# Two more retention heads as seven-product pairs, with their norm in the output product and all head norms' sums on ScalarE

## The chip, the cores and the metric

One core of one Trainium2 chip runs the whole program in one launch. The metric is the device time of that core in microseconds (us), median of the runs shown; lower is better.

## The reference, cut to what matters

```python
# x is (1, 256, 2048) f32; layer 0 is GLA (4 heads), layer 1 retention (8 heads of 512 value columns)
def retention_mixer(h, positions, w_in, gn_g, gn_b, w_out):
    proj = h @ w_in                                   # 2048 -> 2048 q, 2048 k, 4096 v, 4096 gate
    q, k, v, gate = jnp.split(proj, [...], axis=-1)
    ...                                               # rotary, decayed causal scores
    o = ...                                           # scores @ v, per head (256, 512)
    mu = jnp.mean(o, axis=-1, keepdims=True)
    var = jnp.mean(jnp.square(o - mu), axis=-1, keepdims=True)
    o = ((o - mu) * lax.rsqrt(var + EPS)).reshape(B, S, D_INNER)
    o = o * gn_g + gn_b
    return (o * jax.nn.silu(gate)) @ w_out
# h = h + gla_mixer(rms_norm(h, g)); h = h + retention_mixer(rms_norm(h, g)); return rms_norm(h, g)
```

## The kernel before, in words

The 256 tokens stay on the chip and the f32 weights stream past them. A 1 MB "raw" chunk (four buffers, loaded by the SP queue, L192) is cut into two "units". ScalarE rounds a unit to fp32r (`hi`, L218) and VectorE takes the remainder (`lo`, L219), three buffers of each; they are numbered through the program, and the numbering is the order of the weights. A product of TensorE is three matmuls: x-high by hi, x-high by lo, x-low by hi (L358 to L360 in a pair, L267 to L269 in a group).

A plain group (`group_x`, L271) multiplies all 16 k-tiles by both token tiles for one 512-column block: 8 units and 96 matmuls of 512 columns. A seven-product pair (`pair_x`, L340) makes two such blocks together, in Strassen's manner: seven products S1 to S7, each over 4 k-tiles for both column blocks (2 units, 12 matmuls), and the other 8 k-tiles plainly as V0 to V3 and G0 to G3 (1 unit, 12 matmuls each). That is 180 matmuls and 22 units in place of 192 and 16. The sums of weight blocks are made by loads: seven 1 MB loads by SP, and eight 512 KB loads on POOL's queue that accumulate onto a chunk already split (L228, with `then`). A pair needs sums of the tokens as left operand: `token_sums` (L284, VectorE, `*_f` and `*_c`) and `token_parts` (L309, hi by ScalarE and lo by VectorE, `c*_d`).

The order of the blocks is written out by hand in the tables OUT, RET and END (L122 to L126). `plan_all` (L149) lays the units in that order before anything is emitted; `emit_split` (L198) issues splits two units ahead and loads two chunks ahead. Work of a head that is not its weight product waits as generators in the queue `side`; `advance` takes one step of it after each unit or block, and `drain_side` (called in an output pair before V2, as `late`) empties it. A scheduler then fixes each engine's order at build time. PSUM pools: `acc` 4 banks, `lev` 2, `mis` 2.

Retention heads come in two halves: heads 0 to 3 and the output pairs ra0 and ra1, heads 4 to 7 and rb0 and rb1. Each head (`ret_head`, L1242) first makes q and k (`rqk`, a group). Heads 0, 1, 2 and 4, 5, 6 then make value and gate as a pair (`rp0_` ... `rp6_`) in the order RET, and their attention output, norm and gate (`o_part`, `norm_part` L1279, `og_part` L1303) run during the next head's rqk, through `waiting`. Heads 3 and 7 make value and gate as two plain groups (`rv`, `rg`). Their norm runs during rg, from its third unit (`classic`, L1316), which also queues the token sums and splits for the output pairs (`ra_f`, `ra_c`, `c3_d`); their gate multiply and four transposes (`rot`, L692), with the two copies into the output operand `ogt` (L697 hi by ScalarE, L698 lo by VectorE), run at the start of ra0 and rb0, which follow the order OUT. The norm takes mean and variance by VectorE's batch-norm instructions (L1283, L1284) straight from PSUM, and then a scaled subtract (L1285), a Newton reciprocal root of nine tiny steps (`rsqrt`, L482), and a multiply and add.

## Time and profile before

| what | value |
|---|---|
| median of the three runs | 1378.68 us (1377.20 to 1379.46) |
| the profiled execution: its own time | 1378.59 us |
| the span that its trace covers | 1376.8 us |
| mean granted TensorE clock | 0.998 of full speed |
| busy share of the span: TensorE, its weight loads | 99%, 82% |
| busy share: VectorE, ScalarE, POOL | 80%, 60%, 12% |
| loaded and stored | 331.76 MB, mean 241 GB/s |

Busy shares are averages over the whole span. The time lies in the profiled execution 1.8 us outside the span, and 0.09 us below the median. "PE" in rows is TensorE, "PEld" its weight loads, DVE VectorE, ACT ScalarE. An idle time is shown in brackets with what ended it. Successive matmuls overlap, so the distance between the starts of two is their cost, and so it is for VectorE.

### The profile page before, as it was taken

Reading aid. Unit: us, or ns where it says so; the run is one execution under the profiler, and the core shown is the slowest. Engines: PE = TensorE matmul, PEld = TensorE weight load, DVE = VectorE, ACT = ScalarE, POOL = GpSimd, SP = SyncE. Lnnn points to the kernel's source line nnn. Section 1 sums busy time; section 2 is a strip of 40 time slices with the busy share of each in tenths; the row PEclk is TensorE's granted clock in tenths of the full one; section 3 lists DMA queues with packets and bytes.
Section 4 is the critical chain, followed back from the end, with each engine's and each line's share of the span. In section 5 each row is a group of like instructions: output and inputs, shape, how many; then the busy total and the mean of one; then the engine's idle time right before and its main releaser. Section 6 shows DMA issues by size and latency. Waiting matters only on the chain.

```text
span 1376.8 us, 17653 instructions
## 1 busy us (share of the span) xinstructions
PE 1360.3 (99%) x6500; PEld 1132.5 (82%) x6500; DVE 1104.7 (80%) x1517; ACT 831.9 (60%) x1060; POOL 171.9 (12%) x218
## 2 busy tenths in 40 slices
PE   8999999999999999999999999999999999999997
PEld 7888888788878888788888888888888888888876
DVE  6695896888797798887988888878758888887887
ACT  6676666655666766665665656455546465654665
POOL 1011110110122020111011111001201010100210
PEclk9999999999999999999999999999999999999999
DMA  9564785899899695699698969559989797964996
GB/s 366 204 245 163 208 250 186 191 290 321 231 266 277 183 268 195 178 263 278 192 293 265 293 201 286 188 186 262 255 336 226 260 236 251 244 245 163 225 300 168
DMA packets 58871, 331.76 MB, mean 241 GB/s; under 512 B 6928, under 2 KB 7440, under 8 KB 29856
## 3 DMA queue, kind: packets, MB, share of 16 engines
q1 hardware_dynamic: 34656, 238.96, 47.1%
q0 software_dynamic: 23408, 89.01, 33.1%
q10 hardware_dynamic: 720, 2.66, 0.5%
q8 instruction: 51, 0.84, 0.2%
q14 instruction: 36, 0.29, 0.1%
HBM read 324.31 MB, written 6.29 MB: 240 GB/s over the span
## 4 chain that ended last, share of the span: by engine, by line
PE 88%; DVE 5%; DMA 4%; issue 2%; ACT 1%; POOL 0%; ACTq 0%; POOLq 0%; DVEq 0%
PE rqk_ps L464 8%; PE rqk_ps L465 4%; DMA raw<-in_w_all 4%; PE rp__ps L359 4%; PE rp__ps L358 4%; PE rp__ps L360 4%; PE gqk_ps L464 2%; DVE lo L219 2%; PE gp__ps L359 2%; PE gp__ps L360 2%; PE gp__ps L358 2%; PE gv_ps L267 2%; PE gv_ps L268 2%; PE gv_ps L269 2%; PE gg_ps L268 2%; PE gg_ps L267 2%
## 5 line engine op out<-in xcount | busy, mean ns | idle before, releaser
L218 ACT ACTIVATE hi<-raw 128x1024 fp32r<-128x1024 f32 (+1 forms) x585 | 616.9, 1058 | 475.0 <-PE rqk_ps L464 69.0
L219 DVE TENSOR_TENSOR lo<-raw,hi 128x1024 fp32r<-128x1024 f32 (+1 forms) x585 | 709.8, 1223 | 231.3 <-ACT hi L218 222.7
L228 POOL DMA_DIRECT2D raw<-in_w_all x144 | 124.0, 861 | 645.4 <-DVE lo L219 442.5
L464 PE MATMUL rqk_ps<-xhl,hi 128*128 128x512 f32 x480 | 162.6, 397 | 0.0
L465 PE MATMUL rqk_ps<-xhl,lo 128*128 128x256 f32 x480 | 123.3, 281 | 0.0
L464 PEld LDWEIGHTS rqk_ps<-xhl,hi 128*128 128x128 f32 x480 | 88.2, 188 | 17.9
L465 PEld LDWEIGHTS rqk_ps<-xhl,lo 128*128 128x128 f32 x480 | 88.2, 189 | 3.6
L359 PE MATMUL rp__ps<-lo,xhl 128*128 128x512 f32 x192 | 74.9, 390 | 0.0
L360 PE MATMUL rp__ps<-hi,xhl 128*128 128x512 f32 x192 | 74.7, 389 | 0.0
L358 PE MATMUL rp__ps<-hi,xhl 128*128 128x512 f32 x192 | 69.8, 389 | 0.0
L359 PE MATMUL gp__ps<-lo,xhl 128*128 128x512 f32 x128 | 51.0, 399 | 1.5 <-DVE lo L219 1.5
L268 PE MATMUL gv_ps<-lo,xhl 128*128 128x512 f32 x128 | 50.9, 398 | 0.0
L268 PE MATMUL gg_ps<-lo,xhl 128*128 128x512 f32 x128 | 50.1, 392 | 0.0
L269 PE MATMUL gv_ps<-hi,xhl 128*128 128x512 f32 x128 | 50.0, 391 | 0.0
L360 PE MATMUL gp__ps<-hi,xhl 128*128 128x512 f32 x128 | 50.0, 390 | 0.0
L269 PE MATMUL gg_ps<-hi,xhl 128*128 128x512 f32 x128 | 49.8, 389 | 0.0
L464 PE MATMUL gqk_ps<-xhl,hi 128*128 128x512 f32 x144 | 49.6, 398 | 0.0
L358 PE MATMUL gp__ps<-hi,xhl 128*128 128x512 f32 x128 | 47.6, 393 | 0.0
L267 PE MATMUL gg_ps<-hi,xhl 128*128 128x512 f32 x128 | 46.7, 390 | 0.0
L267 PE MATMUL gv_ps<-hi,xhl 128*128 128x512 f32 x128 | 46.2, 393 | 0.0
L359 PEld LDWEIGHTS rp__ps<-lo,xhl 128*128 128x128 f32 x192 | 36.1, 188 | 7.5 <-DVE lo L219 0.3
L358 PEld LDWEIGHTS rp__ps<-hi,xhl 128*128 128x128 f32 x192 | 36.0, 188 | 7.5
(554 smaller groups left out, 2984.4 us busy)
## 6 DMA issues: line engine op xcount, KB each, us to landing
raw<-in_w_all SPq DMA_DIRECT2D x220, 1024.0 KB, 5.9
raw<-in_w_all POOLq DMA_DIRECT2D x144, 512.0 KB, 7.9
ogt<-xc POOLq DMA_DIRECT2D x2, 2048.0 KB, 10.8
resid<-in_x_n SPq DMA_DIRECT2D x2, 1024.0 KB, 10.9
xc<-ogt POOLq DMA_DIRECT2D x1, 2048.0 KB, 9.1
gg<-in_gn_g POOLq DMA_DIRECT2D x8, 256.0 KB, 4.0
gb<-in_gn_b POOLq DMA_DIRECT2D x8, 256.0 KB, 3.9
xc<-ogt ACTq DMA_DIRECT2D x1, 2048.0 KB, 7.3
```

Source lines behind the costliest of these rows:

```text
L218: a = nc.scalar.activation(hi[:, sl], src[:, sl], AF.Copy)
L219: b = nc.vector.tensor_tensor(lo[:, sl], src[:, sl], hi[:, sl].bitcast(F32), ALU.subtract)
L228: nc.gpsimd.dma_start(src, chunk_src(*then)[:, rows], accum_op=ALU.add)
L267: mm(ps, xh, hi[:, q, :], start=kt == 0, stop=False)
L268: mm(ps, xh, lo[:, q, :], start=False, stop=False)
L269: mm(ps, xl, hi[:, q, :], start=False, stop=kt == NKT - 1)
L358: mm(ps, xh, hi[:, q, :], start=start, stop=False, skip_group_check=True)
L359: mm(ps, xh, lo[:, q, :], start=False, stop=False, skip_group_check=True)
L360: mm(ps, xl, hi[:, q, :], start=False, stop=stop, skip_group_check=True)
L464: mm(ps[c], wh, rhs[:, kt, :, :], start=kt == 0, stop=False)
L465: mm(ps[c][:, 0, :], wl, rhs[:, kt, 0, :], start=False, stop=False)
```

## The change

Heads 3 and 7 become pairs too, in the order RET (`rp3_`, `rp7_`). The held gate multiply and transposes of heads 2 and 6 (`held`), the token sums and the first half of the token splits for the output run during that pair; its own norm, gate multiply and transposes run in ra0 and rb0, in the `mis` banks. These two output pairs follow a new order, LATE, which has V2 after S6, and G0 and G1 ahead of it; V2 is the first block that reads the transposed output of head 3 or 7. `load_fn` for columns 0 and 1 moves behind the drained side work. In all eight heads the mean is a ScalarE copy with an accumulated sum (into `o` in SBUF), and the variance a ScalarE square with the mean as bias, written over PSUM with an accumulated sum.

```diff
--- before.py
+++ after.py
@@ -122,6 +122,8 @@
     OUT = ("S1", "S2", "V0", "V1", "S5", "S3", "V2", "G0", "S6", "G1", "S7", "V3", "S4", "G2", "G3")
     RET = ("S1", "V0", "S2", "V1", "S5", "S3", "V2", "G0", "S6", "G1", "S7", "V3", "S4", "G2", "G3")
 
+    LATE = ("S1", "S2", "V0", "V1", "S5", "S3", "G0", "G1", "S6", "V2", "S7", "V3", "S4", "G2", "G3")
+
     END = ("S1", "S2", "V0", "V1", "S5", "S3", "V2", "V3", "G0", "S6", "G1", "G2", "G3", "S7", "S4")
 
     def plan_pair(gp, gq, order):
@@ -151,7 +153,7 @@
         for part, (stage, heads) in enumerate((("gla", 2), ("gla", 2), ("ret", 4), ("ret", 4))):
             for h in range(heads * part, heads * part + heads):
                 plan_group(g)
-                if stage == "ret" and h % heads < heads - 1:
+                if stage == "ret":
                     plan_pair(g + 1, g + 2, RET)
                     g += 3
                     continue
@@ -164,11 +166,10 @@
                         plan_group(g + 4)
                     g += 5
                     continue
-                rest = 4 if stage == "gla" else 2
-                for k in range(1, rest + 1):
+                for k in range(1, 5):
                     plan_group(g + k)
-                g += rest + 1
-            plan_pair(g, g + 1, OUT)
+                g += 5
+            plan_pair(g, g + 1, LATE if stage == "ret" else OUT)
             plan_pair(g + 2, g + 3, END if g + 4 == n_groups else OUT)
             g += 4
 
@@ -306,15 +307,17 @@
                 nc.vector.tensor_tensor(c[:, 1], a11, a21, ALU.add)
             yield
 
-    def token_parts(name, room, keep_in=None):
-        got = []
-        for half in range(2):
+    def token_parts(name, room, keep_in=None, halves=(0, 1)):
+        got = parts.setdefault(name, [])
+        for half in halves:
             c = sums[name][half]
             d = room(half)
             nc.scalar.activation(d[:, 0], c, AF.Copy)
             nc.vector.tensor_tensor(d[:, 1], c, d[:, 0].bitcast(F32), ALU.subtract)
             got.append(d)
             yield
+        if len(got) < 2:
+            return
         combos[name] = tuple((got[i][:, 0, k], got[i][:, 1, k]) for i, k in ((0, 0), (0, 1), (1, 0), (1, 1)))
         if keep_in is not None:
             nc.gpsimd.dma_start(keep_in, ogt[:, 2 * CHUNK :])
@@ -334,8 +337,7 @@
     def temps_t4(name):
         return t4_p.tile([P, CHUNK, SEQ], F32, tag="t4", name=name)
 
-    sums = {}
-    combos = {}
+    sums, parts, combos = {}, {}, {}
 
     def pair_x(lhs, name, cname, on, order, late=None, sparse=False, halves=False):
 
@@ -1001,6 +1003,8 @@
             drain_side()
             side.append(og_part(1))
 
+    waiting = []
+
     def out_cols(c, ps, t, first, final):
         dst = R["t"][:, t, c * GW : (c + 1) * GW]
         nc.vector.tensor_tensor(dst, ps, dst, ALU.add)
@@ -1028,9 +1032,15 @@
         for pair in range(2):
             if pair == 1 and later is not None:
                 side.append(later)
-            for c in (2 * pair, 2 * pair + 1) if final else ():
-                load_fn(c)
-            last = final and pair == 1
+            if last := final and pair == 1:
+                load_fn(2)
+                load_fn(3)
+
+            def whole():
+                drain_side()
+                if final and pair == 0:
+                    load_fn(0)
+                    load_fn(1)
 
             def on(event, ps, shared=True):
                 if final and pair == 0 and event == "21":
@@ -1061,7 +1071,8 @@
                 else:
                     finish(int(event[0]) - 1, 2 * pair + int(event[1]) - 1, ps)
 
-            pair_x(ogt, f"{name}{pair}", name, on, END if last else OUT, drain_side, halves=last)
+            order = END if last else LATE if pair == 0 and name[0] == "r" else OUT
+            pair_x(ogt, f"{name}{pair}", name, on, order, whole, halves=last)
 
     def end_steps():
 
@@ -1237,11 +1248,10 @@
         split_scores(s32, sc)
         box["sc"] = sc
 
-    waiting = []
+    held = []
 
     def ret_head(h):
         hw = {}
-        paired = h % 4 < 3
 
         def late_o(j):
             if j == 0 and waiting:
@@ -1256,8 +1266,8 @@
             token_norm(r2_, "n2")
             nc.vector.tensor_tensor(r2_[:, 1, :], r2_[:, 0, :], r2_[:, 0, :], ALU.mult)
         qk = t4_p.tile([P, 4, SEQ], F32, tag="qk", name=f"rqk{h}", bufs=1)
-        with behind_splits() if paired else nullcontext():
-            evac_w(ps, lambda c: qk[:, c, :], f"rqk{h}", not paired)
+        with behind_splits():
+            evac_w(ps, lambda c: qk[:, c, :], f"rqk{h}", False)
         hw["qk"] = qk
         side.append(ret_scores(h, hw))
         r, r2 = r2_[:, 0, :], r2_[:, 1, :]
@@ -1277,19 +1287,24 @@
             return norm_part(po, o)
 
         def norm_part(po, o):
-            bs = st_p.tile([P, 2, 6], F32, tag="bs", name=f"bs{h}")
-            mv = st_p.tile([P, 2, 2], F32, tag="mv", name=f"mv{h}")
+            st = st_p.tile([P, 3, 2], F32, tag="bs", name=f"bs{h}")
+            total, mean, spread = (st[:, n, :] for n in range(3))
             for t in range(2):
-                nc.vector.bn_stats(bs[:, t, :], po[t])
-                nc.vector.bn_aggr(mv[:, t, :], bs[:, t, :])
+                nc.scalar.activation(o[:, t, :], po[t], AF.Copy, accum_out=total[:, t : t + 1])
+            nc.vector.tensor_scalar(mean, total, -1.0 / GW, None, ALU.mult)
+            yield
+            for t in range(2):
+                nc.scalar.activation(
+                    po[t], o[:, t, :], AF.Square, bias=mean[:, t : t + 1], accum_out=spread[:, t : t + 1]
+                )
                 nc.vector.scalar_tensor_tensor(
-                    o[:, t, :], po[t], mv[:, t, 0:1], gg, ALU.subtract, ALU.mult
+                    o[:, t, :], o[:, t, :], mean[:, t : t + 1], gg, ALU.add, ALU.mult
                 )
                 if t == 0:
                     yield
             m = st_p.tile([P, 2], F32, tag="m", name=f"rm{h}")
             a = st_p.tile([P, 2], F32, tag="hr", name=f"ra_{h}")
-            nc.vector.tensor_tensor(m, mv[:, :, 1], r2, ALU.mult)
+            nc.vector.scalar_tensor_tensor(m, spread, 1.0 / GW, r2, ALU.mult, ALU.mult)
             nc.vector.tensor_scalar(m, m, EPS, None, ALU.add)
             rsqrt(a, m, 2, f"rh{h}")
             nc.vector.tensor_tensor(a, a, r, ALU.mult)
@@ -1309,32 +1324,39 @@
                 lambda t, j: o[:, t, j * P : (j + 1) * P], (h % 4) * 4, None, ogt, f"rot{h}"
             )
 
-        if not paired:
-            v = v_evac(group_x(xhl, f"rv{h}", bank=(lev_p, "lev")), r2, f"rv{h}")
-            load_gn()
-
-            def classic(j):
-                if j == 2:
-                    deque(o_part(v, None, (acc_p, "acc")), maxlen=0)
-                    side.append(token_combos(ogt, "rb" if h == 7 else "ra", room_v(f"c{h}"), temps_t4))
-
-            hw["sg"] = g_evac(group_x(xhl, f"rg{h}", classic), r, f"rsg{h}")
-            side.append(og_part())
-            return
-
         load_gn()
         o = o_p.tile([P, 2, GW], F32, tag="o", name=f"ro{h}")
         sg = sg_p.tile([P, 2, GW], F32, tag="sg", name=f"rsg{h}")
         v = v_p.tile([P, 2, 2, GW], F32R, tag="v", name=f"rv{h}")
 
-        pair_x(xhl, f"rp{h}_", "x1", pair_on(o, sg, v, r, r2), RET)
+        cname, room = ("ra", "rb")[h // 4], room_v(f"c{h}")
+        on = pair_on(o, sg, v, r, r2)
+
+        def on_last(event, *args):
+            on(event, *args)
+            if event == "p2":
+                side.append(held.pop())
+                side.append(token_parts(cname, room, halves=(0,)))
+
+        if h % 4 == 3:
+            side.append(token_sums(ogt, cname, temps_t4))
+        pair_x(xhl, f"rp{h}_", "x1", on_last if h % 4 == 3 else on, RET)
         hw["sg"] = sg
 
         def late():
-            side.append(o_part(v, o, (lev_p, "lev")))
+            if h % 4 < 3:
+                side.append(o_part(v, o, (lev_p, "lev")))
+                (held if h % 4 == 2 else side).append(og_part())
+                return
+            norm = o_part(v, o, (mis_p, "mis"))
+            side.append(token_parts(cname, room, halves=(1,)))
+            side.append(norm)
             side.append(og_part())
 
-        waiting.append(late)
+        if h % 4 < 3:
+            waiting.append(late)
+        else:
+            late()
 
     for h in range(2):
         gla_head(h)
```

The order of the instructions changes as well, since the scheduler places them anew.

VectorE, from the last third of head 3's pair to its first units after the junction with ra0 (lo382 to lo393 are the last units of the pair, lo394 the first of ra0; `ro2`, `rot2` belong to head 2, the held one). Before, around the junction of rg3 with ra0 (lo386 is the first unit of ra0):

```order
L305 TENSOR_TENSOR ra_c1_7886<-ra_f1_7847,ra_c0_7867 128x512
L219 TENSOR_TENSOR lo386_7892<-raw149_7772,hi386_7891 128x1024
L488 SCALAR_TENSOR_TENSOR rh3_nw_7814<-rh3_nw_7814,rm3_7810 128x2
L315 TENSOR_TENSOR c3_d0_7908<-ra_c0_7867,c3_d0_7908 128x1024
L489 TENSOR_TENSOR rh3_nw_7814<-rh3_nw_7814 128x2
L490 SCALAR_TENSOR_TENSOR rh3_nw_7814<-rh3_nw_7814 128x2
L219 TENSOR_TENSOR lo387_7912<-raw149_7772,hi387_7911 128x1024
L315 TENSOR_TENSOR c3_d1_7928<-ra_c1_7886,c3_d1_7928 128x1024
L219 TENSOR_TENSOR lo388_7938<-raw150_7849,hi388_7937 128x1024
L490 SCALAR_TENSOR_TENSOR ra_3_7811<-rh3_nw_7814 128x2
L1044 TENSOR_TENSOR resid_104<-resid_104,ra0_psa_7934 128x512
```

Now:

```order
L220 TENSOR_TENSOR lo389_7818<-raw141_7387,hi389_7817 128x1024
L1321 TENSOR_TENSOR ro2_6985<-ro2_6985,rsg2_6986 128x512 x2
L733 TENSOR_TENSOR ro3_7550<-rp3__ps11_7582,ro3_7550 128x512
L220 TENSOR_TENSOR lo390_7841<-raw147_7675,hi390_7840 128x1024
L496 SCALAR_TENSOR_TENSOR rv3_7552<-ro3_7550,r2_111,rv3_7552 128x512
L700 TENSOR_TENSOR ogt_108<-rot2_tp0_7860,ogt_108 128x2x256
L737 TENSOR_TENSOR ro3_7550<-rp3__ps21_7583,ro3_7550 128x512
L220 TENSOR_TENSOR lo393_7897<-raw148_7687,hi393_7896 128x1024
L742 TENSOR_TENSOR rsg3_7551<-rp3__ps12_7674,rsg3_7551 128x512
L316 TENSOR_TENSOR c3_d0_7917<-ra_c0_7790,c3_d0_7917 128x1024
L496 SCALAR_TENSOR_TENSOR rv3_7552<-ro3_7550,r2_111,rv3_7552 128x512
L220 TENSOR_TENSOR lo394_7935<-raw149_7838,hi394_7934 128x1024
```

Ahead of ra0's first split there now stand the evacuations of the pair (L733 to L742), head 2's gate multiply (L1321) and lo copies (L700), and one token split (L316), between the splits; before, the chain of head 3's tiny norm steps and two token splits stood there.

VectorE in ra0, ahead of V2 (lo406 is V2's unit), now:

```order
L490 SCALAR_TENSOR_TENSOR rh3_nw_8028<-rh3_nw_8028,rm3_8024 128x2
L491 TENSOR_TENSOR rh3_nw_8028<-rh3_nw_8028 128x2
L220 TENSOR_TENSOR lo405_8119<-raw148_7687,hi405_8118 128x1024
L492 SCALAR_TENSOR_TENSOR ra_3_8025<-rh3_nw_8028 128x2
L1310 TENSOR_TENSOR ra_3_8025<-ra_3_8025,r2_111 128x2
L1313 SCALAR_TENSOR_TENSOR ro3_7550<-ro3_7550,ra_3_8025,gb3_7547 128x512 x2
L1321 TENSOR_TENSOR ro3_7550<-ro3_7550,rsg3_7551 128x512
L220 TENSOR_TENSOR lo406_8145<-raw153_8042,hi406_8144 128x1024
L1321 TENSOR_TENSOR ro3_7550<-ro3_7550,rsg3_7551 128x512
L220 TENSOR_TENSOR lo407_8155<-raw151_7932,hi407_8154 128x1024
L700 TENSOR_TENSOR ogt_108<-rot3_tp0_8111,ogt_108 128x2x256
```

Norm steps of head 3 (`rh3`, `ra_3`, `ro3`) stand between the splits up to V2's; before, they ended in the first four units of ra0.

TensorE in ra0, before, where the transposes of head 3 stood inside S5 (units 392 and 393):

```order
L360 MATMUL ra0_ps21_7990<-hi391_7973,ogt_108 128x512
L692 MATMUL rot3_tp0_7983<-ident_103,ro3_7801 128x128
L692 MATMUL rot3_tp1_8008<-ident_103,ro3_7801 128x128
L359 MATMUL ra0_psb_8032<-lo392_7992,c3_d0_7908 128x512
L358 MATMUL ra0_psb_8032<-hi393_8015,c3_d0_7908 128x512
L692 MATMUL rot3_tp0_7983<-ident_103,ro3_7801 128x128 x3
L692 MATMUL rot3_tp1_8008<-ident_103,ro3_7801 128x128 x3
L359 MATMUL ra0_psb_8032<-lo393_8016,c3_d0_7908 128x512
```

Now, at the end of S6 and the start of V2 (unit 406):

```order
L362 MATMUL ra0_psa_7931<-hi405_8118,c3_d0_7917 128x512
L694 MATMUL rot3_tp0_8111<-ident_103,ro3_7550 128x128
L694 MATMUL rot3_tp1_8135<-ident_103,ro3_7550 128x128
L694 MATMUL rot3_tp0_8111<-ident_103,ro3_7550 128x128 x3
L694 MATMUL rot3_tp1_8135<-ident_103,ro3_7550 128x128 x3
L360 MATMUL ra0_ps11_7958<-hi406_8144,ogt_108 128x512
L361 MATMUL ra0_ps11_7958<-lo406_8145,ogt_108 128x512
L360 MATMUL ra0_psa_7931<-hi407_8154,c3_d1_7954 128x512
```

The transposes stand as one block behind S6, and V2's first matmuls right behind them.

## Rows read from the trace of the kernel before

**Rows 1.** The page, parts 1 and 4: busy shares; the chain that ended last.
```profile
PE 1360.3 (99%) x6500; PEld 1132.5 (82%) x6500; DVE 1104.7 (80%) x1517; ACT 831.9 (60%) x1060; POOL 171.9 (12%) x218
...
PE 88%; DVE 5%; DMA 4%; issue 2%; ACT 1%; POOL 0%; ACTq 0%; POOLq 0%; DVEq 0%
```

**Rows 2.** Windows by stage: span, busy PE, PEld, DVE, ACT, POOL, clock, DMA, GB/s.
```profile
813.60:856.80 43.20, 43.20 (x196) 35.90 (x195) 36.86 (x42) 27.54 (x33) 5.70 (x7) 1.00 0.93 265
856.80:881.10 24.30, 24.30 (x142) 21.22 (x141) 19.15 (x37) 11.40 (x15) 1.09 (x2) 1.00 0.59 198
881.10:927.85 46.75, 46.75 (x212) 38.87 (x211) 37.46 (x54) 22.43 (x27) 1.97 (x3) 1.00 0.54 190
927.85:969.00 41.15, 41.11 (x184) 33.46 (x183) 34.54 (x42) 25.00 (x26) 7.47 (x9) 1.00 1.01 274
845.00:855.00 10.00, 10.00 (x46) 8.26 (x45) 8.66 (x10) 7.01 (x8) 0.00 (x0) 1.00 0.98 391
985.00:995.00 10.00, 10.00 (x46) 8.29 (x45) 6.87 (x7) 5.33 (x6) 2.58 (x3) 1.00 1.05 209
```

**Rows 3.** TensorE's timeline in head 6's pair, 14 matmuls apart; columns are start and length.
```profile
1202.00 0.39 PE L358 MATMUL rp__ps<-hi,xhl 128*128 128x512 f32 x1
...
1205.17 0.39 PE L360 MATMUL rp__ps<-hi,xhl 128*128 128x512 f32 x1
```

**Rows 4.** TensorE's timeline at the start of ra0.
```profile
930.57 0.39 PE L358 MATMUL ra_ps<-hi,ogt 128*128 128x512 f32 x1
...
933.37 0.40 PE L358 MATMUL ra_ps<-hi,ogt 128*128 128x512 f32 x1
```

**Rows 5.** All engines' timeline at a block's end in head 2's pair.
```profile
836.84 0.40 PE L359 MATMUL rp__psa<-lo,ogt 128*128 128x512 f32 x1
...
837.04 1.06 ACT L218 ACTIVATE hi<-raw 128x1024 fp32r<-128x1024 f32 x1 [2.17 <-PE rp__psb L360]
...
838.13 1.23 DVE L219 TENSOR_TENSOR lo<-raw,hi 128x1024 fp32r<-128x1024 f32 x1 [0.77 <-ACT hi L218]
...
839.27 0.55 DVE L708 TENSOR_TENSOR rsc<-rs,rsc 128x384 fp32r<-128x384 f32 x1
...
839.74 0.69 DVE L725 TENSOR_TENSOR rsg<-rp__psa,rsg 128x512 f32<-128x512 f32 x1
...
840.34 1.22 DVE L219 TENSOR_TENSOR lo<-raw,hi 128x1024 fp32r<-128x1024 f32 x1
```

**Rows 6.** VectorE's timeline in head 2's pair.
```profile
817.47 1.22 DVE L1209 TENSOR_TENSOR ra<-rqk,trig 128x1024 f32<-128x1024 f32 x1
818.60 1.22 DVE L219 TENSOR_TENSOR lo<-raw,hi 128x1024 fp32r<-128x1024 f32 x1
```

**Rows 7.** All engines' timeline at the junction of two pairs of GLA head 2.
```profile
402.99 0.73 DVE L494 SCALAR_TENSOR_TENSOR gv<-go,rr,gv 128x512 fp32r<-128x512 f32 x1
...
403.65 0.68 DVE L740 TENSOR_TENSOR gsg<-gp__psb,go 128x512 f32<-128x512 f32 x1
...
405.91 0.50 PE L359 MATMUL gp__ps<-lo,xhl 128*128 128x512 f32 x1 [1.48 <-DVE lo L219]
```

**Rows 8.** VectorE's timeline, tiny steps of head 3's norm.
```profile
924.85 0.15 DVE L488 SCALAR_TENSOR_TENSOR rh_nw<-rh_nw,rm 128x2 f32<-128x2 f32 x1
924.92 1.22 DVE L315 TENSOR_TENSOR c_d<-ra_c,c_d 128x1024 fp32r<-128x1024 f32 x1
...
929.02 0.16 DVE L490 SCALAR_TENSOR_TENSOR rh_nw<-rh_nw 128x2 f32<-128x2 f32 x1
929.22 0.16 DVE L488 SCALAR_TENSOR_TENSOR rh_nw<-rh_nw,rm 128x2 f32<-128x2 f32 x1
```

**Rows 9.** ScalarE's squares with sums in GLA heads: ns min, median, max.
```profile
L923 ACT ACTIVATE go_ps<-go x16: 586/602/633, 124.8 to 556.6; 128x512 f32<-128x512 f32 x16
```

**Rows 10.** The waits in ra1: us in total, times, longest.
```profile
ACT hi L218 <- DMA raw<-in_w_all: 8.1, 4, 2.8
...
PE ra_ps L359 <- DVE lo L219: 0.6, 1, 0.6
```

## The prediction

> **What bounds the kernel now.** I read the page first: TensorE is busy for 99% of the span and carries 88% of the chain that ended last [rows 1]. Busy time of overlapping matmuls proves little, so the windows by stage come next [rows 2]. In the pair of head 2, in head 3's q and k group and in its two plain groups TensorE has no idle time at all (43.20 of 43.20, 24.30 of 24.30, 46.75 of 46.75 us), while VectorE has 5 to 9 us idle in each. Ra0 loses 0.04. So time is bought by fewer matmuls, or lost where a split comes late; TensorE's timeline gives the price of a matmul. Between two starts 14 matmuls apart lie 3.17 us [rows 3], 0.2264 us each. The granted clock is 1.00 in all these windows [rows 2], which is the 2.4 GHz level, and nothing in the change leaves TensorE idle for long; I price the clock at nothing.
>
> The Trainium skill, in Perfetto Trace Analysis, Identifying the Most-Contended Engine, calls matmul busy time a poor measure and asks for the busy share of weight loads. Those are busy for 82% of the span here [rows 1] and for 35.90 us over 195 loads in head 2's pair [rows 2], an estimate of 0.184 us each; were that the cost of a matmul, the 24 below would be worth 4.4 us and not 5.4. The pitch of the rows decides.
>
> **The change part by part.** The profiled execution took 1378.59 us, 0.09 under the median; the sum is made against it.
>
> *Matmuls.* In each half, two groups of 96 become a pair of 180: 12 fewer. Twice 12 by 0.2264 us is **-5.43 us**. All of it lies on the path, since TensorE never waits in the two groups [rows 2].
>
> *Splits and evacuations of the new pair.* It has 22 units, the groups 16. In head 2's pair VectorE is busy for 36.86 of 43.20 us and TensorE still never waits [rows 2]; the pair of head 3 carries the same work, with the token sums and head 2's gate multiply in place of part of the norm. Inside the pair: 0. At its end it is another matter.
>
> *The junction of the pair with ra0.* Here evacuations, head 2's gate multiply and lo copies, and one token split stand between the last splits on VectorE. A split cannot run far ahead, since it needs one of three hi buffers: when TensorE ended a unit at 836.84, ScalarE began its next hi 0.20 later and VectorE the lo 1.09 after that [rows 5], 1.29 together. I run VectorE from lo384, the last that such a hand-over certainly starts, to lo394, ra0's first. Distances between starts: a split 1.14 (838.13 to 839.27), a score copy 0.47, a 512-column sum 0.60 [rows 5], a 1024-column one 1.13 [rows 6], a multiply-subtract of 512 columns 0.66 [rows 7]. Lo384 to lo394 are 11 splits, 12.54; 12 sums of 512 columns, 7.2; three multiply-subtracts, 1.98; two of 1024 columns, 2.26; one score copy, 0.47; with the hand-over's 1.29 and 0.09 for the last one's tail, 25.8 us. In that time TensorE has 103 matmuls, 23.3, and eight transposes of 128 columns, which I take at half a matmul's price each, 0.9; together 24.2. It waits **1.6 us**. Bounds: nothing (the groups and head 2's pair show no stall [rows 2]), and 3.0, twice the 1.48 us that the same kind of junction costs in GLA head 2, where evacuations stood ahead of a split [rows 7]. That row is the nearest, so I take 1.6. In return the stall at ra0's start goes: from 930.57 to 933.37 there are ten matmuls in 2.80 us [rows 4], 0.5 more than their price. Net **+1.1** a half.
>
> *Head 3's norm ahead of V2.* The transposes now stand behind S6 and V2's matmuls right behind them. From TensorE's end with unit 398 VectorE needs the hand-over, 1.29; six splits, 6.84; and about 5 us of norm steps and sums: some eight tiny dependent ones of 0.2 (929.02 to 929.22), three of 0.07 between splits (924.85 to 924.92) [rows 8], and five of 512 columns. That is 13.1, against 54 matmuls of TensorE, 12.3: 0.8 late, and V2's first matmuls wait some 0.3 for ScalarE's copy of the transposes. **+1.1** a half. Bounds: nothing, if those steps fill VectorE's idle time (6.6 us in ra0 [rows 2]), and a block, 2.7, if they slip behind one more split pair. Behind the waiting transposes every matmul of V2, S7 and the rest is queued on TensorE, so the wait is paid in full.
>
> *Mean and variance on ScalarE.* Per head two copies with sums and two squares, the squares at about 0.60 us [rows 9] plus reading the sum. For the six paired heads this runs in the next q and k group, where ScalarE is busy 11.40 of 24.30 us and VectorE 19.15 [rows 2]: 0 either way, because TensorE has no wait there to give back. If ScalarE's queue delayed a hi there, the cost would be at most one such operation, 0.6 a head.
>
> *Loads.* Two groups take eight 1 MB loads; a pair takes seven, and eight accumulating 512 KB loads. At 391 GB/s a load takes 2.7 us, at 209 GB/s an accumulating one 2.5 [rows 2]: 38.9 us against 40.8 of matmuls. It fits narrowly: 0. The accumulating loads that the POOL queue gains share it with head 4's bias load, which its wait releases ahead of the loads behind it, and POOL is busy 7.47 us of ra0's 41.15 [rows 2]; SP's order keeps two chunks of lead. If this cover went, see the rival on loads.
>
> **Sum:** -5.43 + 2 x (1.1 + 1.1) = -1.0 us, 1377.6 for the profiled execution, **1377.7** for the median. A measurement tells 0.2%, 2.76 us, from no change; this is inside it.
>
> **The rivals.**
>
> *The cover holds (faster).* VectorE has idle time in all these stages, and the scheduler may have placed the evacuations where their results are awaited least. If neither junction nor norm costs anything and the old 0.5 us stalls go, it is -5.43 - 1.0, 1372.2; with half of my stalls, 1375. For it: head 2's pair, never waiting at 85% of VectorE. Against: the GLA junction, with the same mix of work, did wait [rows 7].
>
> *Loads come late (slower).* Rp3, ra0 and ra1 are now three pairs in a row, where two plain groups gave the queues rest (DMA share 0.54 against 0.93 and 1.01 [rows 2]). In ra1 ScalarE already waits four times for loads, 8.1 us in all, 2.8 the longest, and TensorE pays 0.6 of it [rows 10]. If the row of pairs makes the last of these one longest wait later and TensorE pays it, +2.8 a half: 1377.7 + 5.6 = 1383.3. It decides from 1.9 us a half, where the sum passes +2.76. Against it: the four raw buffers limit how far loads run ahead anyway, so rest earned before ra0 is mostly not stored.
>
> *VectorE pays whole durations (slower).* Each operation above would then cost 0.09 more (a split lasts 1.23, and the next starts after 1.14 [rows 5]): some 28 at the junction and 11 in the chain, 3.5 us a half, 1384.7. The rows speak against it. The Trainium skill's VectorE: DVE Perf Modes, The DRAIN you can't avoid, says that the next operation does not start until the pipe is empty, and that one that is not held starts earlier; the trace agrees with the second part only.
>
> *The change does not act:* the build keeps heads 3 and 7 waiting by as much as the 12 matmuls, 1378.7. The order of instructions does show the pairs, so little speaks for it.
>
> **How the numbers follow.** My forecast 0.50, with its own range 1375.9 to 1379.6; the cover holds 0.34; late loads 0.10; whole durations 0.03; no effect 0.03. The forecast gives 0.48 to no difference and 0.02 to faster; the second case 0.32 to faster, 0.02 to no difference. So faster 0.34, same 0.53, slower 0.13. The range reaches down to 1372.6, nearly to the end of the second case, and up to 1380.9, where each of the four waits of my sum is 0.8 longer; it leaves out the late loads and the whole durations, 0.13, and a little at both edges.
>
> **What would show it.** Right: 24 matmuls fewer, rp3 near 44.0 us where the groups took 46.75, a wait of TensorE for a lo of 1 to 2 us at the junction, and one near 1 us ahead of head 3's transposes, the same in rb0. Wrong: no wait of TensorE at either place (the second case), or idle TensorE behind loads in rp3, ra0 or ra1 of over 2 us a half (the third).

## The result, and the profile after

The changed kernel takes 1388.99 us (median; 1388.46 to 1389.45), the kernel before 1379.22 us beside it: a ratio of 1.0072, 95% interval 1.0060 to 1.0083. It is slower by about 9.8 us. Faster and no change had 0.87 of the chances, and the time lies 8 us above the range and above every rival; the highest of them gave 1384.7. The profiled execution took 1389.27 us, its span is 1387.4.

The page of the changed kernel, parts 1 and 4:

```profile
PE 1361.7 (98%) x6476; PEld 1130.6 (81%) x6476; DVE 1111.3 (80%) x1515; ACT 869.9 (63%) x1142; POOL 185.7 (13%) x234
...
PE 80%; DVE 7%; DMA 7%; issue 3%; ACT 2%; POOL 0%; ACTq 0%; POOLq 0%; DVEq 0%
```

TensorE has 24 matmuls fewer and yet is busy 1.4 us longer, at 98% instead of 99% [rows 1]; its part of the chain fell from 88% to 80%. The busy time is longer because some of its matmuls ran at the slow clock, as the windows below show. The share of the chain does not measure the waits: it is 80% and 79% in runs 1 and 10 below too, where most of them are gone.

Windows of the two kernels tell where. First the halves from head 3's (7's) q and k group to the end of the output pairs, of before (columns as in [rows 2]):

```profile
856.80:1012.50 155.70, 155.03 (x722) 128.42 (x721) 124.17 (x162) 81.96 (x87) 16.56 (x21) 1.00 0.80 238
1212.70:1368.70 156.00, 155.63 (x732) 128.50 (x730) 127.66 (x177) 86.89 (x106) 16.57 (x21) 1.00 0.75 214
```

and of after, with the stages of the first half, and the same place in rb0:

```profile
859.40:1018.90 159.50, 155.47 (x710) 127.89 (x709) 130.44 (x167) 95.25 (x112) 23.45 (x29) 0.98 0.91 252
859.40:882.60 23.20, 23.20 (x133) 20.22 (x132) 15.76 (x31) 13.39 (x21) 1.99 (x3) 1.00 0.66 213
882.60:927.10 44.50, 44.11 (x200) 35.76 (x199) 40.99 (x48) 29.18 (x35) 7.44 (x9) 1.00 0.97 265
927.10:953.80 26.70, 26.70 (x118) 21.58 (x117) 25.63 (x41) 19.86 (x26) 7.13 (x9) 1.00 0.93 223
953.80:958.60 4.80, 1.21 (x9) 0.73 (x7) 3.27 (x5) 1.55 (x3) 0.00 (x0) 0.86 1.05 254
958.60:964.00 5.40, 5.36 (x13) 4.20 (x14) 1.96 (x3) 1.16 (x2) 0.00 (x0) 0.50 1.03 327
...
1219.20:1379.30 160.10, 155.36 (x720) 127.24 (x718) 134.12 (x182) 100.00 (x131) 23.45 (x29) 0.99 0.85 229
1313.20:1319.20 6.00, 1.70 (x11) 0.85 (x9) 4.89 (x7) 2.66 (x4) 0.57 (x1) 0.99 1.06 249
1319.20:1323.00 3.80, 3.80 (x10) 3.04 (x11) 1.91 (x3) 0.42 (x1) 0.00 (x0) 0.56 1.02 305
```

The halves are 3.8 and 4.1 us longer. The rest of the 10.6 us by which the spans differ, 2.7, lies mostly ahead of retention, where both kernels issue the same instructions in the same order: the first retention group began at 654.5 us before and at 656.9 now. It began between 653.7 and 658.1 in all the executions profiled here, with no relation to the edits, so I count it as scatter of single executions.

Inside the half the pair did what it was to do: head 3's stage takes 44.50 us where the two groups took 46.75 [rows 2]. All of the loss is in 953.8 to 964: 4.8 us in which TensorE is busy for 1.21, and 5.4 us at a granted clock of 0.50, the 1.2 GHz level. The same pair of windows stands in rb0. This is V2, the first block that reads head 3's (7's) transposed output. TensorE's timeline there:

```profile
953.75 0.38 PE L694 MATMUL rot_tp<-ident,ro 128*128 128x128 f32 x2
954.93 0.87 PE L694 MATMUL rot_tp<-ident,ro 128*128 128x128 f32 x6 [0.80 <-DVE ro L1321]
958.64 0.79 PE L360 MATMUL ra_ps<-hi,ogt 128*128 128x512 f32 x1 [2.84 <-ACT ogt L699]
959.24 0.63 PE L361 MATMUL ra_ps<-lo,ogt 128*128 128x512 f32 x1
959.66 0.63 PE L360 MATMUL ra_ps<-hi,ogt 128*128 128x512 f32 x1
```

It waits 0.80 us for the second gate multiply in the middle of the transposes, and then 2.84 us for ScalarE's copy of them (L699). The transposes were done by about 955.8. ScalarE's timeline says why the copy came at 958.01:

```profile
951.45 1.06 ACT L219 ACTIVATE hi<-raw 128x1024 fp32r<-128x1024 f32 x1 [1.89 <-PE ra_psb L362]
952.69 1.06 ACT L219 ACTIVATE hi<-raw 128x1024 fp32r<-128x1024 f32 x1 [0.17 <-DMA raw<-in_w_all]
957.05 1.06 ACT L219 ACTIVATE hi<-raw 128x1024 fp32r<-128x1024 f32 x1 [3.30 <-DMA raw<-in_w_all]
958.01 1.06 ACT L699 ACTIVATE ogt<-rot_tp 128x512 fp32r<-128x512 f32 x2
```

Between them stands hi408, the split of S7's second unit, and it waits 3.30 us for its weights. The order of ScalarE's instructions shows that the build had put it there:

```order
L219 ACTIVATE hi407_8154<-raw151_7932 128x1024
L219 ACTIVATE hi408_8165<-raw151_7932 128x1024
L699 ACTIVATE ogt_108<-rot3_tp0_8111 128x2x256
L699 ACTIVATE ogt_108<-rot3_tp1_8135 128x2x256
```

The weights are a sum that POOL's second accumulating load for S7 completes. It was issued at 944.3, and the DMA view of that instant (line, queue, count, KB, us from issue to landing) gives its flight, then that of the 1 MB load that SP issued 2.7 us later and that feeds only the last blocks of ra0, and last the same accumulating load in the kernel before:

```profile
raw<-in_w_all POOLq DMA_DIRECT2D x1, 512.0 KB, 12.6
```
```profile
raw<-in_w_all SPq DMA_DIRECT2D x1, 1024.0 KB, 10.1
```
```profile
raw<-in_w_all POOLq DMA_DIRECT2D x1, 512.0 KB, 9.6
```

12.6 us against 9.6. In the kernel before, SP issued no load between 936.4 and 953.9. My reading is that LATE splits G0 and G1 earlier, so that their raw buffer is free earlier and the next load starts earlier, beside the one that is needed; runs 7 and 9 try it.

So there are three theories. **Queue:** V2 waits because the copy stands on ScalarE behind a split that waits for a load. **Late load:** the load itself holds TensorE, wherever the copy stands. **Norm:** the norm chain, now with two passes through ScalarE, is what is late.

### The profile page after: what moved, and what is told of

It reads as the page before. It is cut to its first block, busy times and chain, and to the rows that moved or that the text cites. A ratio compares the mean times of both kernels' runs of the same rounds, so it can differ in the third digit from the quotient of the medians.

```text
span 1387.4 us, 17750 instructions
## 1 busy us (share of the span) xinstructions
PE 1361.7 (98%) x6476; PEld 1130.6 (81%) x6476; DVE 1111.3 (80%) x1515; ACT 869.9 (63%) x1142; POOL 185.7 (13%) x234
## 4 chain that ended last, share of the span: by engine, by line
PE 80%; DVE 7%; DMA 7%; issue 3%; ACT 2%; POOL 0%; ACTq 0%; POOLq 0%; DVEq 0%
PE rqk_ps L466 8%; DMA raw<-in_w_all 6%; DVE lo L220 4%; PE rqk_ps L467 4%; PE rp__ps L361 4%; PE rp__ps L362 4%; PE rp__ps L360 4%; PE gqk_ps L466 2%; PE gv_ps L269 2%; PE gv_ps L268 2%; PE gv_ps L270 2%; PE gp__ps L361 2%; PE gp__ps L362 2%; PE gp__ps L360 2%; PE gg_ps L269 2%
## 5 line engine op out<-in xcount | busy, mean ns | idle before, releaser
L220 DVE TENSOR_TENSOR lo<-raw,hi 128x1024 fp32r<-128x1024 f32 (+1 forms) x597 | 724.1, 1224 | 243.6 <-ACT hi L219 236.5
L219 ACT ACTIVATE hi<-raw 128x1024 fp32r<-128x1024 f32 (+1 forms) x597 | 629.5, 1058 | 442.9 <-PE rqk_ps L466 53.4
L229 POOL DMA_DIRECT2D raw<-in_w_all x160 | 137.7, 860 | 734.3 <-DVE lo L220 534.9
L467 PE MATMUL rqk_ps<-xhl,lo 128*128 128x256 f32 x480 | 126.1, 280 | 0.0
L361 PE MATMUL rp__ps<-lo,xhl 128*128 128x512 f32 x256 | 100.7, 393 | 0.7 <-DVE lo L220 0.6
L362 PE MATMUL rp__ps<-hi,xhl 128*128 128x512 f32 x256 | 99.8, 390 | 0.0
L360 PE MATMUL rp__ps<-hi,xhl 128*128 128x512 f32 x256 | 93.2, 390 | 0.0
L361 PEld LDWEIGHTS rp__ps<-lo,xhl 128*128 128x128 f32 x256 | 48.1, 188 | 13.5 <-DVE lo L220 4.0
L360 PEld LDWEIGHTS rp__ps<-hi,xhl 128*128 128x128 f32 x256 | 48.1, 188 | 10.2 <-ACT hi L219 0.2
L362 PEld LDWEIGHTS rp__ps<-hi,xhl 128*128 128x128 f32 x256 | 48.1, 188 | 9.8
L270 PE MATMUL gv_ps<-hi,xhl 128*128 128x512 f32 x128 | 50.0, 391 | 0.0
## 6 DMA issues: line engine op xcount, KB each, us to landing
resid<-in_x_n SPq DMA_DIRECT2D x2, 1024.0 KB, 10.7
```

The source lines that it names most:

```text
L219: a = nc.scalar.activation(hi[:, sl], src[:, sl], AF.Copy)
L220: b = nc.vector.tensor_tensor(lo[:, sl], src[:, sl], hi[:, sl].bitcast(F32), ALU.subtract)
L229: nc.gpsimd.dma_start(src, chunk_src(*then)[:, rows], accum_op=ALU.add)
L270: mm(ps, xl, hi[:, q, :], start=False, stop=kt == NKT - 1)
L360: mm(ps, xh, hi[:, q, :], start=start, stop=False, skip_group_check=True)
L361: mm(ps, xh, lo[:, q, :], start=False, stop=False, skip_group_check=True)
```

## The experiments

All are edits of the changed kernel unless said otherwise, with the code shortened where `...` stands. Each ratio is to the kernel before, run beside them on the same chip; its medians were 1379.22 us for runs 1 to 4, 1378.33 for runs 5 to 8 and 1379.49 for runs 9 to 11.

**1. The copies ahead of the waiting split.**

```diff
+    def behind_copies():                    # around the split issued from V2's block
+        ...
+        with tc.issue_after(a), tc.issue_after(b):
+            yield
...
-                nc.scalar.activation(d[:, :, 0, :], tp, AF.Copy)
-                nc.vector.tensor_tensor(d[:, :, 1, :], tp, d[:, :, 0, :].bitcast(F32), ALU.subtract)
+                a = nc.scalar.activation(d[:, :, 0, :], tp, AF.Copy)
+                b = nc.vector.tensor_tensor(d[:, :, 1, :], tp, d[:, :, 0, :].bitcast(F32), ALU.subtract)
```

> The changed kernel, with ScalarE's and VectorE's copies of head 3's and 7's transposes put ahead of the split of S7's second unit (hi408, lo408 and their twins) instead of behind it; nothing else. Queue theory (V2 waits because its operand's copy stands on ScalarE behind a split that itself waits for a late accumulating load): TensorE's wait at V2 falls from 4.0 and 4.8 us to under 1.5 and 2.5, the granted clock stays at 1.00 there, and the time falls to 1377 to 1382 us. Late-load theory (the load itself holds TensorE): the wait only moves to S7's second unit, the time stays within 2 us of 1389. Norm theory (the norm chain through ScalarE is what is late): the wait for the transposes stays, at most 3 us gained in all.

Measured 1380.41 us, ratio 1.0009 (0.9999 to 1.0019). One exchange of places on two engines takes back 8.6 of the 9.8 us. ScalarE's timeline of this run:

```profile
950.20 1.06 ACT L219 ACTIVATE hi<-raw 128x1024 fp32r<-128x1024 f32 x1 [0.58 <-DMA raw<-in_w_all]
953.00 1.08 ACT L711 ACTIVATE ogt<-rot_tp 128x512 fp32r<-128x512 f32 x2 [1.74 <-PE rot_tp L706]
954.37 1.06 ACT L219 ACTIVATE hi<-raw 128x1024 fp32r<-128x1024 f32 x1 [0.28 <-DMA raw<-in_w_all]
```

The late-load theory falls: TensorE does not wait at S7's second unit instead. The copies now wait for the transposes and nothing else, and the split that follows waits only 0.28 for its load. TensorE waits 1.18 and 0.36 us at this place in ra0, and its clock stays up; in rb0 the clock fell all the same, as the windows of this run show, two in ra0 and two in rb0:

```profile
950.90:953.60 2.70, 1.21 (x9) 0.74 (x7) 2.70 (x4) 0.96 (x3) 0.00 (x0) 1.00 1.04 288
953.60:960.00 6.40, 6.35 (x28) 5.27 (x29) 4.99 (x6) 4.25 (x5) 0.00 (x0) 1.00 1.05 266
1305.70:1309.30 3.60, 1.86 (x11) 0.97 (x11) 3.60 (x5) 1.82 (x3) 0.57 (x1) 1.00 1.04 280
1309.30:1313.00 3.70, 3.70 (x10) 2.90 (x11) 2.76 (x4) 1.39 (x2) 0.00 (x0) 0.55 1.06 211
```

**2. The norm's statistics back on VectorE** (`bn_stats`, `bn_aggr` and the subtract from PSUM, in all eight heads).

```diff
-                nc.scalar.activation(o[:, t, :], po[t], AF.Copy, accum_out=total[:, t : t + 1])
...
-                nc.scalar.activation(
-                    po[t], o[:, t, :], AF.Square, bias=mean[:, t : t + 1], accum_out=spread[:, t : t + 1]
-                )
+                nc.vector.bn_stats(bs[:, t, :], po[t])
+                nc.vector.bn_aggr(mv[:, t, :], bs[:, t, :])
...
```

> The changed kernel with mean and variance of the retention heads back on VectorE's batch-norm instructions. Queue theory: the split with the late load still stands ahead of the copies, so V2 still waits 3 to 5 us a half: 1387 to 1391 us. Norm theory: the transposes come 1 to 3 us earlier in each half and the idle time before V2 shrinks with them: 1380 to 1384 us. Late-load theory: no change, 1389.

Measured 1389.60 us, 1388.76 without one execution of 1503.14, which the ratio leaves out as well: 1.0070 (1.0053 to 1.0087). The waits from 950 to 960 (us in total, times, longest) are the same three:

```profile
ACT hi L219 <- DMA raw<-in_w_all: 4.2, 2, 2.6
...
PE ra_ps L360 <- ACT ogt L699: 2.2, 1, 2.2
...
PE rot_tp L694 <- DVE ro L1316: 2.0, 2, 1.3
```

The norm theory falls as the cause of the loss: with the two passes off ScalarE the time is the same. What waits for the end of the norm chain itself are the transposes, 0.8 us in ra0 and 1.9 in rb0 in the changed kernel, and that wait is left in run 1 (1.2 and 1.3).

**3. That part alone, in the kernel before.** Edit 2 turned round, on the kernel before.

> The kernel before with only the part on ScalarE's mean and variance, all eight heads. Queue theory and late-load theory: hidden, within 1.5 us of 1379. Norm theory: it costs something of its own where heads 3 and 7 are normed inside their gate group, 1381 to 1384 us.

Measured 1379.60 us, ratio 1.0003 (0.9994 to 1.0013). The part is hidden, as the prediction had it.

**4. Without S7's sum in ra0 and rb0.** S7 takes the chunk as it is, so this kernel leaves out a part of the output products.

```diff
-                plan_units(c, n in (4, 7), {1: (gq, 0), 5: (gq, 1), 6: (gp, 1), 3: (gq, 0)}.get(n))
+                then = {1: (gq, 0), 5: (gq, 1), 6: (gp, 1), 3: (gq, 0)}.get(n)
+                plan_units(c, n in (4, 7), None if n in skip else then)   # skip: 3 in ra0, rb0
```

> The changed kernel without the two accumulating loads (512 KB each) that make S7's weight sum in ra0 and rb0; S7 there takes the unsummed chunk, so the output pairs' result changes. Both the queue theory and the late-load theory: nothing ahead of the copies waits for a load any more, V2's wait falls under 1.5 and 2.5 us, the clock stays up, 1376 to 1381 us. If this is much faster than the run with the copies ahead, the load itself costs too; if both are alike, it cost only through the queue. Norm theory: no gain over 3 us.

Measured 1379.36 us, ratio 0.9995 (0.9984 to 1.0005). TensorE's waits at V2, 950 to 960 in this run's list of waits, are those of run 1:

```profile
PE rot_tp L695 <- DVE ro L1322: 1.0, 1, 1.0
...
PE ra_ps L361 <- ACT ogt L700: 0.4, 1, 0.4
```

With the load gone (4) or its wait moved behind the copies (1) the times lie 1 us apart: nearly all that the late load cost, it cost through ScalarE's queue.

**5. The gate multiplies too.** Run 1, with VectorE's split of V2's unit behind both gate multiplies, where it had stood between them.

```diff
-                b = nc.vector.tensor_tensor(lo[:, sl], src[:, sl], hi[:, sl].bitcast(F32), ALU.subtract)
+                with behind_gate(i):        # V2's unit: tc.issue_after(second gate multiply)
+                    b = nc.vector.tensor_tensor(lo[:, sl], src[:, sl], hi[:, sl].bitcast(F32), ALU.subtract)
```

> The run with the copies ahead, and beside it VectorE's split of V2's own unit put behind both gate multiplies of head 3 and 7 (before, it stood between the two). Queue theory: the wait for the second multiply, 1.2 to 1.3 us in each half, shrinks to about 0.2, and the granted clock stays at 1.00 in rb0 too, where it had fallen for 3 us: 1376 to 1379 us, faster than the kernel before. Late-load theory: TensorE then waits for S7's second unit instead, no gain, 1380.

Measured 1380.52 us, ratio 1.0018 (1.0007 to 1.0028): no gain on run 1 by these times. The granted clock stays at 1.00 in rb0. The waits of rb0, 1308 to 1315:

```profile
PE rb_psa L377 <- ACT hi L221: 0.6, 1, 0.6
PE rb_psa L377 <- DVE resid L1074: 0.4, 1, 0.4
...
PE rb_ps L377 <- ACT ogt L717: 0.4, 1, 0.4
PE rot_tp L712 <- DVE ro L1341: 0.2, 1, 0.2
```

The wait for the multiply went to 0.2. In its place S7 waits 0.4 for VectorE, which joins S6's result later (`resid`), and 0.6 for ScalarE's split of its second unit, which still waits for its load: 1.0 together. The clock that stays up does show in the profiled execution: the second half, 1214.2 to 1370.7, takes 156.50 us, where run 1's, 1211.8 to 1369.6, takes 157.80. But this execution came to retention 3.5 us later than run 1's (657.2 against 653.7), and such scatter hides a gain of that size.

**6. No wait for the norm.** The eight transposes of heads 3 and 7 read the constant identity and not the head's output, so this kernel leaves two heads out of the output products.

```diff
-                lambda t, j: o[:, t, j * P : (j + 1) * P], (h % 4) * 4, None, ogt, f"rot{h}"
+                lambda t, j: ident if h % 4 == 3 else o[:, t, j * P : (j + 1) * P],
+                (h % 4) * 4, None, ogt, f"rot{h}"
```

> The changed kernel, with head 3's and 7's eight transposes each taken from the constant identity instead of the gated output, so that nothing before V2 waits for the norm chain; the chain itself, the copies and all loads are still made, and the output pairs' result changes. It shows what the change is worth without that wait. Sum of the prediction without its norm term: -5.4 for the matmuls, the junctions at the 0.8 us a half that the changed kernel's trace shows, 0.4 a half of old stalls gone: 1374 to 1377 us. Late-load theory: V2 no longer covers the load of S7's second unit, TensorE waits there 1 to 2 us a half, 1377 to 1380 us.

Measured 1378.11 us, ratio 0.9992 (0.9984 to 1.0001). Here nothing before V2 waits for the norm, and what is left of the gain is 0.2 us by the medians and 1.1 by the ratio, whose interval just reaches no change. By its windows the first half takes 153.40 us against 155.70, a gain of 2.3, and the second 155.20 against 156.00, a gain of 0.8:

```profile
859.20:1012.60 153.40, 152.89 (x710) 125.95 (x709) 130.36 (x167) 95.21 (x112) 23.46 (x29) 1.00 0.93 261
1212.90:1368.10 155.20, 153.90 (x720) 125.99 (x718) 134.06 (x182) 99.84 (x131) 23.45 (x29) 1.00 0.87 235
```

That is 3.1 in the halves; this execution began retention at 656.7 us, 2.2 later than the one of the kernel before, so its span is only 0.6 shorter.

**7. The old order.** OUT in ra0 and rb0.

```diff
-            plan_pair(g, g + 1, LATE if stage == "ret" else OUT)
+            plan_pair(g, g + 1, OUT)
...
-            order = END if last else LATE if pair == 0 and name[0] == "r" else OUT
+            order = END if last else OUT
```

> The changed kernel with the output order OUT in ra0 and rb0 in place of LATE: V2 planned ahead of S6 and G0. Queue theory: the copies then stand behind hi407, the first unit of S7, and V2's unit holds one of three hi buffers through S6, so splits come just in time: V2 waits as long as now or longer, 1387 to 1395 us. Late-load theory: the raw buffers come free later, no early 1 MB load competes with S7's sum, 1380 to 1386 us.

Measured 1382.72 us, ratio 1.0023 (1.0012 to 1.0033). The queue theory's number is wrong here: OUT is better than LATE by 6 us, and the time lies in the range that the late load gave. TensorE waits for splits now, as the waits of rb0 (1282 to 1312) show; my reading is that V2's unit, planned early, holds one of three hi buffers until the transposes come:

```profile
PE rb_psa L360 <- ACT hi L219: 1.7, 1, 1.7
...
PE rb_ps L360 <- ACT hi L219: 1.2, 2, 0.7
```

That is 2.9 us (1.6 in ra0), where LATE waits 4.3 (3.6) for the multiply and the copies, and the clock falls in rb0 only. That the hi buffer binds is argued from the order and not tried by an edit. The load of S7's second sum shows the other half of the difference. With OUT, SP issues no load between 935.9 and 953.6, and the sum's load, issued at 943.1, lands 10.5 us later and not 12.6, by the DMA view of that instant:

```profile
raw<-in_w_all POOLq DMA_DIRECT2D x1, 512.0 KB, 10.5
```

How much of the 6 us is the load and how much the place of the copies, this run does not separate.

**8. V2 behind S7.**

```diff
-    LATE = ("S1", "S2", "V0", "V1", "S5", "S3", "G0", "G1", "S6", "V2", "S7", "V3", "S4", "G2", "G3")
+    LATE = ("S1", "S2", "V0", "V1", "S5", "S3", "G0", "G1", "S6", "S7", "V2", "V3", "S4", "G2", "G3")
```

> The changed kernel with V2 one block later in LATE, behind S7. The scheduler still places the transposes and V2's first two matmuls ahead of S7 on TensorE, and the copies behind both splits of S7 and the one of V2 on ScalarE. Queue theory: nothing gained, one more split ahead of the copies: 1388 to 1394 us. Norm theory: one block more time for the chain, 1383 to 1386 us.

Measured 1393.16 us (five executions, 1389.78 to 1394.38), ratio 1.0102 (1.0089 to 1.0115). Nothing is gained, as the queue theory has it, and the norm theory's 1383 to 1386 is missed. That the 4 us more are the price of one more split is not shown. The waits of ra0 (945 to 965) in the profiled execution, which took 1391.01, are these:

```profile
PE ra_ps L360 <- ACT ogt L699: 2.9, 1, 2.9
...
PE rot_tp L694 <- DVE ro L1321: 1.9, 1, 1.9
```

The wait for the copies grew by 0.0 in ra0 and by 0.9 in rb0 (3.3); the other 1.1 of longer waits in ra0 is for the second gate multiply.

**9. The competing load behind the sums.**

```diff
-            nc.sync.dma_start(t[:, sl, :], src[:, sl, :])
+            (nc.gpsimd if c in behind_sums else nc.sync).dma_start(t[:, sl, :], src[:, sl, :])
...                                         # behind_sums: the chunk of G2 and G3 in ra0 and rb0
```

> The changed kernel, with the one 1 MB load in ra0 and rb0 that feeds their last blocks G2 and G3 issued on POOL's queue, behind the two accumulating loads of S7's sum, instead of by SP beside them. Competition theory (LATE frees a raw buffer earlier, the 1 MB load starts at 947, and S7's second sum lands late because it shares the engines with it): that sum lands 1.5 to 3 us earlier than 12.6 us after its issue, ScalarE's copies follow, V2's wait falls by as much, the clock falls for a shorter time: 1381 to 1386 us. Plain bandwidth theory (the sums are late because all loads since the pair before queue up): landing within 1 us of now, 1387 to 1391 us.

Measured 1381.55 us, ratio 1.0008 (0.9998 to 1.0017). The load of S7's second sum lands 10.7 us after its issue, not 12.6, by the DMA view of that instant:

```profile
raw<-in_w_all POOLq DMA_DIRECT2D x1, 512.0 KB, 10.7
```

In rb0 it is 11.0 against 13.5 (10.4 in the kernel before). ScalarE's wait for it fell to 1.41 us, its split is over before the last transpose, and the copy follows with no wait for the split:

```profile
956.16 1.06 ACT L222 ACTIVATE hi<-raw 128x1024 fp32r<-128x1024 f32 x1 [1.41 <-DMA raw<-in_w_all]
957.42 1.08 ACT L702 ACTIVATE ogt<-rot_tp 128x512 fp32r<-128x512 f32 x2 [0.20 <-PE rot_tp L697]
```

Nothing about the queue was changed here; 2 us of flight made the difference between 0.36 and 2.84 us of waiting and the slow clock. The start of that load beside the sum is shown as the cause of 1.9 of the 3.0 us of lateness in ra0, and run 7, where it starts later for another reason, agrees (10.5); the plain bandwidth theory would have left the landing where it was. The other 1.1 is open. One candidate stands in the traces: in the changed kernel POOL's queue carries head 4's bias load (`gb`, 256 KB) between these accumulating loads, issued at 941.18 and landing at 949.4, 1.2 us behind the load ahead of it. It stands there in runs 7 and 9 too, and not in the kernel before. No run took it out.

**10 and 11. Together.** Run 1 with 9, and run 5 with 9.

> Copies ahead and that load behind the sums, together. Competition theory: nothing in ra0 and rb0 waits for a load, what is left is the wait for the second gate multiply, 1.3 us a half: 1377 to 1380 us. Plain bandwidth theory: as with the copies ahead alone, 1380 to 1381 us.

> Copies ahead, the gate multiplies ahead of V2's split, and that load behind the sums. If the waits that are left are independent, the best version: 1375 to 1378 us, under the kernel before. If the gate's gain is only taken back by the join of S6 and by S7's splits, as in the run without the load moved: 1379 to 1381 us.

Measured 1379.90 us, ratio 0.9999 (0.9989 to 1.0010), and 1379.42 us, ratio 1.0003 (0.9994 to 1.0012). Both stand level with the kernel before. Run 11 was to reach 1375 to 1378 if the waits that are left were independent; it did not.

## Why the prediction was wrong

*Matmuls, -5.43:* right. Head 3's stage is 2.25 us shorter and contains 0.84 of new waits, 3.1 together for the 2.7 of a half.

*Junction, 1.6 of wait a half:* right in kind, half in size. TensorE's starts are 0.48 and 0.36 us late behind 914.28 and 921.42, 0.84 in all, and 0.77 in the other half, in the last blocks of the pair; the bounds held it. A name was wrong there and in the words on the order of instructions: ra0's first unit is 392, the pair's last 391 (386 before, and six units more), so the run from lo384 to lo394 reaches two units into ra0.

*Norm ahead of V2, 1.1 a half:* **this step failed.** Its 0.8 for the chain (0.9, since 54 matmuls at 0.2264 are 12.2 and not 12.3) was nearly right in ra0 (0.96 late) and well under half in rb0 (2.2). Its 0.3 "for ScalarE's copy of the transposes" is 0.52 when the copy's way is free (run 1: 0.36 of it idle) and was 3.0 and 2.6. The copy was priced as if nothing stood ahead of it on ScalarE; the order of instructions, argued from for VectorE and TensorE only, had hi408 there. The upper bound, a block of 2.7, was put on VectorE's steps, and on no queue that a load can stop.

*Loads, 0:* wrong in the way that mattered. I compared totals, 38.9 of 40.8 us, and found that they fit. One load was late by 3 us, and run 9 gives 1.9 of that to the start of another load, which LATE had moved ahead. The bias load that the prediction names in the same paragraph may be part of the rest; no run shows it. The rival on late loads had the right cause in the wrong place: it looked at the last loads in ra1, and there the waits became shorter (from 0.6 us for TensorE [rows 10] to none that the waits list). It missed that a late load can cost through an instruction that does not use it.

*The clock, nothing:* wrong as a consequence. The starts at 959.24 and 959.66 are 0.42 apart, at 0.2264 otherwise [rows 3]; eleven such steps cost 2.2 us in ra0, and six 1.2 in rb0. The prediction priced it at nothing because it saw no long idle time coming.

The half with ra0 then adds up: -2.7 for matmuls, +0.8 junction, +4.0 at V2, +0.4 for the first matmul behind the wait, +2.2 clock, and -0.5 and -0.6 for the old waits at ra0's start and in ra1 that are gone [rows 4, 10]: +3.6 of the 3.8 that the windows show.

*Mean and variance on ScalarE, 0:* right (run 3). *VectorE at whole durations:* nothing of it. Another 0.09 us for each of some 28 operations would have made the junction dearer than 1.6 us by 2.5; 0.84 was measured. The Trainium skill, in VectorE: DVE Perf Modes, The DRAIN you can't avoid, says that the next operation does not start until the pipe is empty, and that one that is not held starts earlier; this trace agrees with the second part only. In ra0 of the changed kernel a split of 1.22 us starts at 953.06 and the next operation at 954.19.

The forecast of no change came near a kernel that has the copies in the other order: 1380.41 against 1377.7, and 1379.42 at the best. Part of that nearness is luck: by run 1's windows the first half takes 154.60 us, 1.1 less than before, and the second 157.80, 1.8 more, where the sum had half a microsecond less for each. What is left of the gain when the wait is gone is less sure: run 6 measured 1378.11 where the same sum without the norm gave 1374 to 1377. Its two halves gain 3.1 us where the terms of that sum make 4.6; waits for splits of 0.9 us in rb0 and rb1, where the kernel before lists 0.2, are a part of what is missing. The other 2 us of that execution lie ahead of retention; that they are scatter is argued, not shown.

## What to carry to other kernels

When a value goes through an engine between producer and consumer, price the wait by what stands ahead of it in that engine's queue, and ask of each such instruction which load it waits for: here a late load cost nearly all of its price through an innocent instruction behind it, and exchanging the two took back 8.6 of 9.8 us. A new order of blocks also moves the releases of buffers, and so the starts of loads; look for the transfer that now flies beside the one that is needed. Totals of bytes per stage do not show either.

## What was not expected of the hardware

Behind stretches of 4.8 and 6.0 us in which TensorE was busy for 1.21 and 1.70, the granted clock was 0.50 for 5.4 us and 0.56 for 3.8. That is the low level of 1.2 GHz: the starts there are 0.42 us apart and not 0.2264. But in rb0 of run 1 it fell behind 3.6 us with 1.86 busy, and in run 9 it did not, in ra0 or rb0, behind as much:

```profile
954.50:958.10 3.60, 1.80 (x12) 0.91 (x10) 3.60 (x5) 2.00 (x4) 0.57 (x1) 1.00 1.01 345
958.10:963.00 4.90, 4.90 (x22) 4.05 (x23) 3.99 (x6) 2.44 (x3) 0.00 (x0) 1.00 1.07 263
1310.60:1314.20 3.60, 1.79 (x11) 0.89 (x9) 3.60 (x5) 2.11 (x4) 0.57 (x1) 1.00 1.04 350
1314.20:1319.00 4.80, 4.80 (x21) 4.00 (x22) 3.88 (x6) 2.34 (x3) 0.00 (x0) 1.00 1.05 247
```

The transposes and first matmuls of V2 start at nearly the same distances in these three places (the long gap is 1.74 us in each). So neither the length of the wait nor the busy time in it decided it alone, and what did is open.
